# Four places in a queue: when a gated-DeltaNet layer's values, gate row, keys' turns and a late rsqrt are issued

## The chip, the cores and the metric

The kernel runs on one core of one Trainium2 chip. The metric is the device time of one execution in microseconds (us). The engines go by the profile's names: PE is TensorE (PEld its weight loads), DVE VectorE, ACT ScalarE, POOL GpSimd, SP the engine whose queue issues most DMAs. Each engine works through its own queue in order, so an instruction that waits holds up all that stands behind it on that engine.

## What is computed

One layer of a diffusion backbone over 1024 latent tokens and 256 context tokens of width 1024. After a modulated norm, one input projection feeds eight heads of neighbourhood attention and four heads of a gated DeltaNet. A branch's output is multiplied by a gate, and both go through one output projection. What the change touches is the DeltaNet's front, cut here to its core:

```python
def gdn_qkv(qkv, conv_w):                 # qkv: columns of the input projection
    qkv = short_conv(qkv, conv_w)         # 5 taps per channel, then silu
    q, k, v = jnp.split(qkv, ...)         # 4 heads of 128 each
    return l2norm(q), l2norm(k), v        # then axial rope on latent q and k

# gated_delta_chunked, per head and chunk of 64 tokens
a = jnp.where(lower, (k * beta) @ k.T * decay, 0.0)
t_inv = solve_triangular(eye + a, eye)    # unit lower triangle
u, w = t_inv @ (v * beta), t_inv @ (k * beta * exp(gc))
qk = (q @ k.T) * decay                    # then a scan over the chunks
```

## The kernel before

The kernel has stages one behind the other. Up to some 115 us it builds the modulated norm `hh`/`hl` (the input split in two parts, so that a product is three matmuls: high by high, low by high, high by low) and begins the projections. From there to some 435 us runs `phase2`, in which the DeltaNet's heads 0 to 3 are prepared. From 435 to 552 us, which is called the merges' stage below, the small inverses are put together (`tz`, `tu`, `tm`) between the last projections (`na_proj` of pairs 2 and 3). Attention and scan follow up to some 780 us and the output product up to the end.

In `phase2` each head h takes the steps of a string. Q and K (`conv`): 48 matmuls each of 512 columns of the projection (`gpl`), and for keys the context's (`gpc`); then five taps on ACT and DVE (`acc`, line 887), a tanh on ACT (line 888) and the multiply that ends the silu on DVE (line 889). F (`delta_front`) is the decay matrix of the head before: `em` from a DMA through ACT, `pk` on PE, `pm` and `qe` on DVE. Then `"RVppTppUB"`: R is the residual gate's row (`res_gate`: `parg` on PE, a copy `growg` on ACT, the product `pg` on PE, line 427), V the values' conv, p one piece of other projections as filler, T (`qk_tok`) the turning of queries and keys into token rows (`tp` on PE, line 909), with a copy and squares on ACT (line 915), one rsqrt on POOL (`rq_y_g`, lines 169 and 170: an add and a power) and the rotation on POOL and DVE (lines 921 to 933; `tok`). U turns the values (`vtp`, line 826), B (`qk_back`) turns the rotated keys and queries back (`tb`, line 944). From head 2 on a generator of triangular inversions is woven in: `tb`/`vb` on DVE (lines 1078 and 1081), 31 steps of two instructions each, over group 0 (head 0 and half of head 1) in head 2 and over group 1 in head 3. Group 2 follows in the merges' stage (`ab_vv`). The name `tb` thus stands for a DVE scratch at line 1078 and a PSUM tile at line 944.

The program's text is not the order of the queues. A scheduler with a simulated timeline places the instructions of each engine by priority and by what its model says of readiness; `self.order(r, before)` adds an edge without a semaphore, so that r comes behind another instruction of the same queue. Tiles come from pools with a count of buffers: two for `xp`, three for `acc`, three for the PSUM tiles `tp`, `pg` and `pk` together, two for `pm` and for `qe`.

The only place in which the kernel before uses such an edge on PE in the projections is in the stage ahead of `phase2`: `self.after` holds one matmul of a projection behind the last of the products that pick rows for the norm (`pa`, line 310).

## Time and profile before

| | |
|---|---|
| median of 3 runs | 872.3 us (871.33 to 875.08) |
| profiled execution | 871.71 us, of which the trace's span is 869.9 us |
| mean granted PE clock | 0.972 |
| PE busy | 824.9 us (95%) |
| PE's weight loads | 696.4 us (80%) |
| DVE busy | 502.7 us (58%) |
| ACT busy | 417.3 us (48%) |
| POOL busy | 357.3 us (41%) |
| chain that ended last | PE 59%, DVE 16%, DMA 15%, issue 4% |

A row of a timeline reads: start, duration, engine, line, operation, output and inputs, how many instructions are drawn together, and in brackets the idle time of the engine just before it with what ended it. The granted clock (PEclk) is the share of full speed that TensorE got in a stretch: 1.00 is 2.4 GHz and 0.50 is 1.2 GHz. The 1.8 us between span and execution lie around the traced work and belong to no stage.

### The profile page before, as it was taken

What the parts mean: (1) busy time and instruction counts of PE and PEld (TensorE: products, weight loads), DVE (VectorE), ACT (ScalarE), POOL (GpSimd) and SP (SyncE); (2) the same over time, 40 slices, a digit from 0 to 9 for tenths busy, and PEclk for the clock granted to TensorE, in tenths of its full rate; (3) what the DMA queues carried; (4) which work ended last, traced back from release to release, by engine and by line L of the source; (5) the groups of instructions that cost most, each with busy time, mean ns of one, the idle gap of its engine ahead of it and who ended that gap; (6) DMA issues with size and microseconds to landing.
All of it is one profiled execution on the core that took longest, in us unless ns stands there. A gap on an engine that the chain in (4) does not pass through costs nothing.

```text
span 869.9 us, 16461 instructions
## 1 busy us (share of the span) xinstructions
PE 824.9 (95%) x6082; PEld 696.4 (80%) x6082; DVE 502.7 (58%) x1051; ACT 417.3 (48%) x1087; POOL 357.3 (41%) x430
## 2 busy tenths in 40 slices
PE   6999999999999989989898999899999999999996
PEld 3678887888788867769786788788898988878885
DVE  3444455536743699859935964456666655653342
ACT  5244334753664643355314334366666667734210
POOL 2224141453462553328262100655757559624110
PEclk9999999999999999989998999699999999999999
DMA  8778352255444825562597569995967925134251
GB/s 340 265 259 295 97 170 88 73 170 168 142 157 154 221 85 170 176 171 81 176 283 226 160 187 290 419 258 149 313 179 262 259 78 191 49 110 133 87 184 69
DMA packets 86054, 159.65 MB, mean 184 GB/s; under 512 B 18373, under 2 KB 45334, under 8 KB 83798
## 3 DMA queue, kind: packets, MB, share of 16 engines
q1 hardware_dynamic: 78486, 144.94, 53.0%
q10 hardware_dynamic: 7488, 13.67, 5.1%
q8 instruction: 48, 0.79, 0.4%
q14 instruction: 32, 0.26, 0.1%
HBM read 109.51 MB, written 52.42 MB: 186 GB/s over the span
## 4 chain that ended last, share of the span: by engine, by line
PE 59%; DVE 16%; DMA 15%; issue 4%; ACT 2%; POOL 2%; SPq 1%; DVEq 0%; POOLq 0%; ACTq 0%
PE py L1369 3%; PE py L1370 3%; PE py L1371 3%; DVE tb L1078 3%; DVE vb L1081 3%; PE pa L1260 2%; PE pz L463 2%; PE pz L468 2%; PE pz L467 2%; PE po L789 2%; DMA wada<-in_w_ada 2%; PE pa L1271 2%; PE po L784 2%; DMA pm_dram<-pm 2%; PE tr L772 2%
## 5 line engine op out<-in xcount | busy, mean ns | idle before, releaser
L759 ACT ACTIVATE pt<-pt,nm 128x544 f32<-128x544 f32 (+1 forms) x64 | 50.5, 790 | 37.5 <-DVE nm L758 37.0
L758 DVE CUSTOM_DVE_ANT_0 pt<-sc,gm 128x544 f32<-128x544 f32 (+1 forms) x64 | 49.4, 771 | 32.2 <-PE sc L754 25.8
L742 POOL TENSOR_TENSOR gm<-gt,mk 128x288 f32<-128x288 f32 (+1 forms) x48 | 46.5, 971 | 29.1 <-DVE nm L758 28.8
L1232 POOL TENSOR_SCALAR kd<-kt,kd 128x128 f32<-128x128 f32 x72 | 42.7, 605 | 20.5 <-PE pa L1271 19.9
L1020 ACT ACTIVATE em<-em,gc 128x128 f32<-128x128 f32 x80 | 25.5, 391 | 34.9 <-DMA em<-gc_dram 29.7
L467 PE MATMUL pz<-hl,wh_gz 128*128 128x512 f32 x96 | 38.6, 402 | 0.0
L463 PE MATMUL pz<-hh,wh_gz 128*128 128x512 f32 x96 | 38.3, 399 | 0.0
L468 PE MATMUL pz<-hh,wl_gz 128*128 128x512 f32 x96 | 38.2, 398 | 0.0
L476 PE MATMUL pv<-wh_nv,hh 128*128 128x264 f32 x128 | 35.5, 296 | 2.0 <-ACT hh L265 1.7
L477 PE MATMUL pv<-wh_nv,hl 128*128 128x264 f32 x128 | 36.8, 292 | 0.0
L1431 DVE TENSOR_TENSOR finv<-py,ggb 128x512 f32<-128x512 f32 x16 | 10.9, 689 | 43.2 <-ACT finv L1430 43.1
L478 PE MATMUL pv<-wl_nv,hh 128*128 128x264 f32 x128 | 35.6, 287 | 0.0
L1274 DVE SCALAR_TENSOR_TENSOR s<-s,egl,pa 128x128 f32<-128x128 f32 x64 | 19.6, 344 | 27.2 <-PE pa L1271 27.2
L1039 POOL TENSOR_SCALAR_AFFINE_SELECT qe<-qe 128x256 f32<-128x256 f32 x32 | 25.5, 800 | 24.1 <-DVE qe L1038 24.1
L887 DVE SCALAR_TENSOR_TENSOR acc_v<-xp_v,cols,acc_v 128x1282 f32<-128x1282 f32 x16 | 29.1, 1817 | 10.9 <-ACT acc_v L885 10.6
L1078 DVE TENSOR_TENSOR tb<-ab,vb 120x31 f32<-120x31 f32 (+15 forms) x62 | 30.2, 487 | 8.7 <-DMA ab<-ab_dram 7.1
L1137 POOL COPY tm<-ld 32x320 f32<-32x320 f32 x16 | 7.4, 464 | 65.0 <-DMA tm_dram<-tm 27.1
L1430 ACT ACTIVATE finv<-py 128x512 f32<-128x512 f32 x16 | 9.5, 597 | 48.6 <-PE py L1371 30.5
L1238 POOL TENSOR_SCALAR vb<-v,beta 128x128 f32<-128x128 f32 x40 | 24.2, 604 | 20.4 <-DVE y L1244 17.2
L772 PE MATMUL tr<-c,pt 128*96 128x128 f32 (+1 forms) x192 | 31.8, 275 | 0.0
L1035 DVE SCALAR_TENSOR_TENSOR pm<-pk,beta,em 128x128 f32<-128x128 f32 x80 | 23.5, 342 | 14.0 <-PE pk L1028 10.9
L770 ACT COPY tcx<-tc 128x256 f32<-128x256 f32 x64 | 23.4, 366 | 16.2 <-PE tc L768 15.8
(432 smaller groups left out, 2852.7 us busy)
## 6 DMA issues: line engine op xcount, KB each, us to landing
wada<-in_w_ada SPq DMA_DIRECT2D x16, 512.0 KB
em<-gc_dram SPq DMA_DIRECT2D x20, 256.0 KB
pm_dram<-pm SPq DMA_DIRECT2D x20, 256.0 KB
tm_dram<-tm SPq DMA_DIRECT2D x8, 640.0 KB
kk<-qk_dram SPq DMA_DIRECT2D x16, 320.0 KB
tm<-tm_dram SPq DMA_DIRECT2D x4, 1280.0 KB
kq_dram<-kq SPq DMA_DIRECT2D x4, 1152.0 KB
kq<-kq_dram SPq DMA_DIRECT2D x4, 1152.0 KB
```

What stands on the lines that cost most here:

```text
L463: r = nc.tensor.matmul(ps, wh, xh, start=(k == 0), stop=False)
L467: nc.tensor.matmul(ps, wh, xl, start=False, stop=False)
L468: nc.tensor.matmul(ps, wl, xh, start=False, stop=(k == KC - 1))
L476: nc.tensor.matmul(ps, xh, wh, start=(k == 0), stop=False)
L477: nc.tensor.matmul(ps, xl, wh, start=False, stop=False)
L478: nc.tensor.matmul(ps, xh, wl, start=False, stop=(k == KC - 1))
L742: r = nc.gpsimd.tensor_tensor(self.gm[hh][:, 384 - n:384].rearrange("p (n c r) -> p n c r", c=nco, r=4), gv, self.mk[:, mo:mo + n].rearran ...
L758: nc.vector.tensor_tensor_reduce(pt[:, 384 - n:], sc[:, 512 - n:768], gm[:, 384 - n:], -1.0, 3.0e38, ALU.add, ALU.min, nm)
L759: self.last_exp = nc.scalar.activation(pt[:, 384 - n:], pt[:, 384 - n:], AF.Exp, bias=nm, scale=-1.0, accum_out=sums[:, ct, hh:hh + 1]).in ...
L772: self.pe(nc.tensor.transpose(pl[:m, rc * P:(rc + 1) * P], pt[:, 384 + (rc - 3) * m:384 + (rc - 2) * m], self.ident))
L1078: nc.vector.tensor_tensor(t3, bc(ab[:, 0:m, m:m + 1], [r, m, n]), bc(vb[:, m:m + 1, m:], [r, m, n]), ALU.mult)
L1232: r = nc.gpsimd.tensor_scalar(kd[d], kt_[:, t, :], self.kd[:, h, d, t:t + 1], None, ALU.mult)
```

## The change

Five things are edited, four of them by an edge in a queue.

1. The values' silu is split off `conv` (`late=True` gives back a function) and issued in a step of its own, "v", behind T. Its tanh is put behind the last of the head's squares on ACT (`last_sq`). The multiply that ends it is now line 910.
2. `res_gate` becomes a generator. Its product `pg` is issued in a step "r" behind V, with an edge behind the last matmul of the projections issued by then (`last_mm`).
3. The turns back (`tb`, now line 969) get an edge behind the `last_mm` of that moment.
4. The rsqrt over all heads' queries (`rho`), which only the scan uses, gets an edge behind the fourth head's `rq_y_g3` on POOL.
5. A wrapper `mm` issues the projections' matmuls and keeps the name of the last one; with it the use of `self.after` is gone, so that the edge in the stage ahead of `phase2` is gone as well.

No operation is added or removed on any engine. The scheduler sets all queues anew, so more rows move than those named.

```diff
+    def mm(self, *a, **k):
+        r = self.nc.tensor.matmul(*a, **k)
+        self.last_mm = r.ins.name
+        if self.seq:
+            self.pe(r)
...
-    def rsqrt(self, pool, x, n, tag, eps):
+    def rsqrt(self, pool, x, n, tag, eps, behind=None):
         y = pool.tile([P, n], F32, name=f"rq_y_{tag}", tag=f"rq_y{n}")
-        self.nc.gpsimd.tensor_scalar(y, x, eps, None, ALU.add)
-        self.nc.gpsimd.tensor_tensor(y, y, bc(self.mhalf, [P, n]), ALU.pow)
+        r = self.nc.gpsimd.tensor_scalar(y, x, eps, None, ALU.add)
+        if behind:
+            self.order(r, behind)
+        self.last_rsqrt = self.nc.gpsimd.tensor_tensor(y, y, bc(self.mhalf, [P, n]), ALU.pow).ins.name
...
         nc.scalar.copy(rows, par)
+        yield
...
-        nc.tensor.matmul(pg[:1, :256], self.sel[:, 0:1], rows, start=True, stop=True)
+        self.order(nc.tensor.matmul(pg[:1, :256], self.sel[:, 0:1], rows, start=True, stop=True), self.last_mm)
...
-            r = nc.tensor.matmul(ps, wh, xh, start=(k == 0), stop=False)
-            if self.after:
-                self.order(r, self.after)
-                self.after = None
+            self.mm(ps, wh, xh, start=(k == 0), stop=False)
...
-                for c in "RVppTppUB":
+                for c in "RVrppTvppUB":
...
-        nc.scalar.activation(xp[:, s0:1282], av, AF.Tanh, scale=0.5)
-        nc.vector.scalar_tensor_tensor(av, xp[:, s0:1282], 1.0, av, ALU.add, ALU.mult)
+        def silu():
+            r = nc.scalar.activation(xp[:, s0:1282], av, AF.Tanh, scale=0.5)
+            if late:
+                self.order(r, self.last_sq)
+            nc.vector.scalar_tensor_tensor(av, xp[:, s0:1282], 1.0, av, ALU.add, ALU.mult)
...
+        behind = self.last_mm
...
-                nc.tensor.transpose(pb[:, t, :], tok[:, t, :], self.ident)
+                self.order(nc.tensor.transpose(pb[:, t, :], tok[:, t, :], self.ident), behind)
...
-            self.rho = self.rsqrt(self.cp, self.ssq.rearrange("p h t -> p (h t)"), 32, "rho", 4 * EPS)
+            self.rho = self.rsqrt(self.cp, self.ssq.rearrange("p h t -> p (h t)"), 32, "rho", 4 * EPS,
+                                  self.last_rsqrt)
```

DVE in head 2, before: the multiply that ends the values' silu (`acc_v2`, line 889) stands early among the inversion steps of group 0 (`tb0`, `vb0`).

```order
L1078 TENSOR_TENSOR tb0_2755<-ab0_2752,vb0_2754 120x156
L1081 TENSOR_TENSOR vb0_2754<-vb0_2754,tb0_2755 120x26x6
L889 SCALAR_TENSOR_TENSOR acc_v2_2769<-xp_v2_2768,acc_v2_2769 128x1282
L1078 TENSOR_TENSOR tb0_2755<-ab0_2752,vb0_2754 120x175
L1081 TENSOR_TENSOR vb0_2754<-vb0_2754,tb0_2755 120x25x7
```

DVE in head 2, after:

```order
L1106 TENSOR_TENSOR vb0_2746<-vb0_2746,tb0_2747 120x18x14
L1103 TENSOR_TENSOR tb0_2747<-ab0_2744,vb0_2746 120x255
L910 SCALAR_TENSOR_TENSOR acc_v2_2761<-xp_v2_2760,acc_v2_2761 128x1282
L1106 TENSOR_TENSOR vb0_2746<-vb0_2746,tb0_2747 120x17x15
L565 SCALAR_TENSOR_TENSOR st_z10_3131<-st_z10_3131,pz1_0_3106 128x512
L945 TENSOR_TENSOR tok2_0_0_2996<-tp2_0_0_2993,rq_y_g2_3029 128x256
```

The multiply has moved from behind the step of 156 elements to behind that of 255, past 17 instructions of the inversion, and stands now just ahead of the keys' `tok2`.

PE at the values' turns of head 2 (`vtp2_0`, `vtp2_2`), before: they stand right behind the last filler product `pz1_0`.

```order
L467 MATMUL pz1_0_3094<-hl_113,wh_gz1_4_3089 128x512
L468 MATMUL pz1_0_3094<-hh_112,wl_gz1_4_3090 128x512
L826 MATMUL vtp2_0_3129<-c128_60,acc_v2_2769 128x128 x2
L826 MATMUL vtp2_2_3135<-c128_60,acc_v2_2769 128x128 x4
L463 MATMUL gpl_q30_3212<-hh_112,wh_gq3_0_3197 128x512
```

PE at the same place, after:

```order
L157 MATMUL gpl_q30_3224<-hh_112,wh_gq3_4_3215 128x512
L157 MATMUL gpl_q30_3224<-hl_113,wh_gq3_4_3215 128x512
L843 MATMUL vtp2_0_3141<-c128_60,acc_v2_2761 128x128 x2
L843 MATMUL vtp2_2_3147<-c128_60,acc_v2_2761 128x128 x4
L157 MATMUL gpl_q30_3224<-hh_112,wl_gq3_4_3216 128x512
```

The turns have moved behind 23 of the 24 products `gpl_q30` of the next head's queries.

POOL in head 3, before: the power of `rho` stands ahead of both instructions of `rq_y_g3`, which the keys' `tok3` needs.

```order
L169 TENSOR_SCALAR rq_y_rho_5749<-ssq_1091 128x32
L933 TENSOR_TENSOR tok3_1_6_3781<-tok3_1_6_3781,rot3_16_3795 128x512
L170 TENSOR_TENSOR rq_y_rho_5749<-rq_y_rho_5749,mhalf_67 128x32
L169 TENSOR_SCALAR rq_y_g3_3836<-ss3_3799 128x10
L1192 TENSOR_TENSOR rho2_5752<-rq_y_rho_5749 128x32
L170 TENSOR_TENSOR rq_y_g3_3836<-rq_y_g3_3836,mhalf_67 128x10
```

POOL in head 3, after:

```order
L957 TENSOR_TENSOR tok3_1_6_3785<-tok3_1_6_3785,rot3_16_3799 128x512
L177 TENSOR_SCALAR rq_y_g3_3840<-ss3_3803 128x10
L180 TENSOR_TENSOR rq_y_g3_3840<-rq_y_g3_3840,mhalf_67 128x10
L177 TENSOR_SCALAR rq_y_rho_5749<-ssq_1091 128x32
L180 TENSOR_TENSOR rq_y_rho_5749<-rq_y_rho_5749,mhalf_67 128x32
L1218 TENSOR_TENSOR rho2_5752<-rq_y_rho_5749 128x32
```

The two instructions of `rq_y_g3` now come first. On DVE `acc_v3`'s multiply stands behind the step of 252 elements of group 1, where before it stood behind that of 156, and `tok3` follows one row later.

DVE at the start of the merges' stage, after: the transposes `vx`, `vd`, `ld` (32 by 32 blocks) of merges 0 and 1 stand ahead of the first step of group 2; before, they stand between its steps, from the fourth on.

```order
L538 TENSOR_TENSOR sl_k22_4461<-pk2_2_4435,sh_k22_4460 128x256
L1139 STREAM_TRANSPOSE vx0_4405<-vl0_4387 128x1024
L1140 STREAM_TRANSPOSE vd0_4403<-vx0_4405 128x640
L1141 STREAM_TRANSPOSE ld0_4404<-vd0_4403 128x640
L1139 STREAM_TRANSPOSE vx1_4607<-vl1_4388 128x1024
L1140 STREAM_TRANSPOSE vd1_4421<-vx1_4607 128x640
L538 TENSOR_TENSOR sl_k20_4641<-pk2_0_4615,sh_k20_4640 128x512
L1141 STREAM_TRANSPOSE ld1_4422<-vd1_4421 128x640
L1103 TENSOR_TENSOR tb2_qh0_4370<-ab_vv_4368 80x31
```

On PE the first merge's `tz0`, which reads `ld0`, has moved ahead by 33 products of the filler, and between the last merges stand 48 products of the filler where 21 stood.

## Rows read from the trace of the kernel before

**Rows 1.** The page's first part: busy us (share of the span) and instructions

```profile
PE 824.9 (95%) x6082; PEld 696.4 (80%) x6082; DVE 502.7 (58%) x1051; ACT 417.3 (48%) x1087; POOL 357.3 (41%) x430
```

**Rows 2.** Waits of PE, 300 to 440 us: us in total, times, longest

```profile
PE tb L944 <- DVE tok L921: 4.3, 2, 2.9
PE tp L909 <- ACT sq L915: 3.3, 1, 3.3
PE pg L427 <- ACT growg L421: 2.9, 1, 2.9
PE gpc_v L468 <- POOL wl_gv L449: 0.4, 1, 0.4
```

**Rows 3.** Stretches: length, busy us of PE, PEld, DVE, ACT, POOL, clock, DMA, GB/s

```profile
320.00:325.00 5.00, 5.00 (x20) 4.20 (x21) 4.93 (x4) 4.75 (x23) 4.54 (x7) 0.70 0.29 106
375.00:385.00 10.00, 10.00 (x31) 7.36 (x32) 4.19 (x5) 8.09 (x16) 2.84 (x2) 0.70 0.62 144
435.00:552.00 117.00, 108.57 (x1432) 90.51 (x1431) 66.98 (x146) 39.92 (x85) 30.80 (x45) 0.91 0.80 243
```

**Rows 4.** Timeline of ACT and PE around head 2's wait for the squares

```profile
317.94 1.27 ACT L888 ACTIVATE xp_v<-acc_v 128x1282 f32<-128x1282 f32 x1 [7.44 <-DVE acc_v L887]
...
319.93 1.12 PE L909 MATMUL tp<-c,acc_k 128*128 128x128 f32 x4 [3.26 <-ACT sq L915]
...
326.21 0.82 PE L826 MATMUL vtp<-c,acc_v 128*128 128x128 f32 x6
...
327.33 0.39 PE L468 MATMUL gpl_q<-hh,wl_gq 128*128 128x512 f32 x1
327.56 0.39 PE L463 MATMUL gpl_q<-hh,wh_gq 128*128 128x512 f32 x1
...
334.03 0.41 PE L944 MATMUL tb<-c,tok 128*128 128x128 f32 x2 [1.44 <-DVE tok L921]
```

**Rows 5.** Timeline of DVE and POOL in head 2's inversion (group 0)

```profile
319.56 1.49 DVE L889 SCALAR_TENSOR_TENSOR acc_v<-xp_v,acc_v 128x1282 f32<-128x1282 f32 x1
320.96 1.42 DVE L1078 TENSOR_TENSOR tb<-ab,vb 120x175 f32<-120x175 f32 x1
...
326.50 0.38 DVE L1078 TENSOR_TENSOR tb<-ab,vb 120x207 f32<-120x207 f32 x1
...
332.19 0.42 DVE L1078 TENSOR_TENSOR tb<-ab,vb 120x255 f32<-120x255 f32 x1
...
322.22 1.30 POOL L933 TENSOR_TENSOR tok<-tok,rot 128x512 f32<-128x512 f32 x1
```

**Rows 6.** Timelines of DVE, PE and POOL in head 3

```profile
387.38 0.21 DVE L1078 TENSOR_TENSOR tb<-ab,vb 120x31 f32<-120x31 f32 x1 [3.74 <-DMA ab<-ab_dram]
...
401.02 2.58 DVE L889 SCALAR_TENSOR_TENSOR acc_v<-xp_v,acc_v 128x1282 f32<-128x1282 f32 x1
...
403.88 1.34 DVE L1078 TENSOR_TENSOR tb<-ab,vb 120x175 f32<-120x175 f32 x1
...
411.18 0.42 DVE L1081 TENSOR_TENSOR vb<-vb,tb 120x252 f32<-120x252 f32 x1
...
416.53 1.01 DVE L921 TENSOR_TENSOR tok<-tp,rq_y_g 128x256 f32<-128x256 f32 x2
...
407.75 0.82 PE L826 MATMUL vtp<-c,acc_v 128*128 128x128 f32 x6
...
404.98 5.55 POOL L170 TENSOR_TENSOR rq_y_rho<-rq_y_rho,mhalf 128x32 f32<-128x32 f32 x1
```

**Rows 7.** Timeline of PE ahead of `phase2`

```profile
53.55 0.75 PE L476 MATMUL pv<-wh_nv,hh 128*128 128x264 f32 x4 [0.94 <-ACT hh L265]
```

**Rows 8.** Timeline of DVE in the merges' stage

```profile
462.51 0.20 DVE L1078 TENSOR_TENSOR tb_qh<-ab_vv 80x31 f32<-80x31 f32 x1 [11.92 <-DMA ab_vv<-ab_dram]
...
465.40 1.25 DVE L1114 STREAM_TRANSPOSE vx<-vl 128x1024 f32<-128x1024 f32 x1 [1.07 <-DMA qk_dram<-sl_k]
...
467.32 1.26 DVE L1115 STREAM_TRANSPOSE vd<-vx 128x640 f32<-128x640 f32 x1
...
468.68 0.83 DVE L1116 STREAM_TRANSPOSE ld<-vd 128x640 f32<-128x640 f32 x1
...
510.51 0.19 DVE L1081 TENSOR_TENSOR ab_vv<-ab_vv,tb_qh 80x31 f32<-80x31 f32 x1
```

More of the change, by code (lines that the diff above doesn't have):

```diff
@@ L147, in __init__ @@
         self.gm = {}
-        self.gate = self.after = None
+        self.gate = self.last_pe = self.last_hh = None
+        self.seq = False
     def order(self, r, before):
@@ L431, in res_gate @@
         nc.sync.dma_start(self.gg_dram[:, n:n + 256], br[:, 0, :])
+        yield
     def load_w(self, pool, c0, n, tag, bufs=(3, 4, 4), halves=2, load=None, ks=None, dst=None):
@@ L462, in mm_chan @@
                 xh, xl = (v.rearrange("p (a t c) -> p t a c", a=8, t=4) for v in (xh, xl))
-            r = nc.tensor.matmul(ps, wh, xh, start=(k == 0), stop=False)
-            if self.after:
-                self.order(r, self.after)
-                self.after = None
-            nc.tensor.matmul(ps, wh, xl, start=False, stop=False)
-            nc.tensor.matmul(ps, wl, xh, start=False, stop=(k == KC - 1))
+            self.mm(ps, wh, xh, start=(k == 0), stop=False)
+            self.mm(ps, wh, xl, start=False, stop=False)
+            self.mm(ps, wl, xh, start=False, stop=(k == KC - 1))
     def mm_tok(self, ps, w, c0, n, xsel, ks=range(KC)):
@@ L475, in mm_tok @@
             xh, xl = xsel(k)
-            nc.tensor.matmul(ps, xh, wh, start=(k == 0), stop=False)
-            nc.tensor.matmul(ps, xl, wh, start=False, stop=False)
-            nc.tensor.matmul(ps, xh, wl, start=False, stop=(k == KC - 1))
+            self.mm(ps, xh, wh, start=(k == 0), stop=False)
+            self.mm(ps, xl, wh, start=False, stop=False)
+            self.mm(ps, xh, wl, start=False, stop=(k == KC - 1))
     def nat_tok(self, t):
@@ L802, in phase2 @@
             self.fill, self.ready = self.projections(cv), []
-            kq, conv, toks = {}, {}, {}
+            kq, conv, toks, gate_row = {}, {}, {}, None
             def step(h, c):
+                nonlocal gate_row
                 if c in "QKV":
                     i = "QKV".index(c)
-                    conv[c] = self.conv(cv, ps, 4 * i + h, f"{'qkv'[i]}{h}", i > 0)
+                    conv[c] = self.conv(cv, ps, 4 * i + h, f"{'qkv'[i]}{h}", i > 0, c == "V")
+                    if c == "V":
+                        conv[c], conv["v"] = conv[c]
+                elif c == "v":
+                    conv.pop("v")()
+                elif c == "r":
+                    next(gate_row)
                 elif c == "p":
@@ L815, in step @@
                 elif c == "R":
-                    self.res_gate(cv, ps, h)
+                    gate_row = self.res_gate(cv, ps, h)
+                    next(gate_row)
                 elif c == "T":
@@ L862, in projections, with conv @@
         yield from self.na_proj(pool, self.ps, [2, 3])
-    def conv(self, cv, ps, chunk, tag, has_ctx):
+    def conv(self, cv, ps, chunk, tag, has_ctx, late=False):
         nc = self.nc
@@ L887, in conv @@
             nc.vector.scalar_tensor_tensor(av, xp[:, s0 + tap:s0 + tap + 1282 - s0], wc(tap), av, ALU.mult, ALU.add)
-        nc.scalar.activation(xp[:, s0:1282], av, AF.Tanh, scale=0.5)
-        nc.vector.scalar_tensor_tensor(av, xp[:, s0:1282], 1.0, av, ALU.add, ALU.mult)
+        def silu():
[3 more added lines that the diff above has]
+            nc.vector.scalar_tensor_tensor(av, xp[:, s0:1282], 1.0, av, ALU.add, ALU.mult)
+        if late:
+            return acc, silu
+        silu()
         return acc
@@ L914, in qk_tok @@
                     sq = cv.tile([P, P], F32, name=f"sq{h}_{which}{t0 + t}", tag="sq", bufs=1)
-                    nc.scalar.activation(sq, pt[:, t, :], AF.Square,
-                                         accum_out=ss[:, t0 + t - first:t0 + t - first + 1])
+                    self.last_sq = nc.scalar.activation(sq, pt[:, t, :], AF.Square,
+                                                        accum_out=ss[:, t0 + t - first:t0 + t - first + 1]).ins.name
                 pts.append((t0, n, pt, tok))
```

## Prediction

> **What bounds the kernel now.** The page's busy times come first: TensorE works 95% of the span and no other engine over 58% [rows 1], so time is won only where TensorE stands still or runs at half its clock. The list of its waits says where that is in the stage that the change edits: four waits of 3.3, 2.9, 1.4 and 2.9 us and one of 0.4, together 10.9 us [rows 2]. Behind two of them it also loses clock: 320 to 325 us was granted 0.70, so 1.5 us are lost, and 375 to 385 us 0.70, so 3.0 [rows 3]. The merges' stage has more to give: in 117 us TensorE is busy for 108.6, so it stands for 8.4, and at a mean clock of 0.91 it loses another 10.5 [rows 3]. Then each wait is followed to the engine that ends it. The 3.26 us at 319.93 wait for squares on ACT, and ACT had stood for 7.44 us at the values' tanh, which waited for DVE [rows 4]. The 2.86 us at 417 wait for `tok3` at 416.53, and the rsqrt that it needs stood on POOL behind a power of 5.55 us for `rho`, which only the scan uses [rows 2, 6]. So all four orders aim at real waits. What the reader should look at next is DVE: in head 2 it has no gap from 319.56 to past 332, in head 3 none from 387.38 to 418 [rows 5, 6].
>
> **The change part by part.** I sum against the profiled execution of 871.7 us, which lies 0.6 under the median.
>
> *Ahead of `phase2`.* With the edge of `self.after` gone, six products of 0.23 us [rows 4] come before the row-picking matmuls, so these and the `hh` that follows from them on ACT are 1.4 us later. TensorE already waits 0.94 us for an `hh` there [rows 7]. Nothing new covers it: +1.2 us, from 0 (the six products fill a hole) to 2.5 (a second wait, for the context's norm, whose transposes also move ahead).
>
> *Head 2.* The squares no longer stand behind the tanh: the 3.26 us and the 1.5 of clock go. The 1.44 us at the turns back go too, since `tok2` is ready at about the old time and TensorE reaches its turns later in its queue. But the tanh takes the multiply of `acc_v2` along, and the order puts that behind 17 more instructions of the inversion, with `vtp2` waiting for it. Before, DVE worked without a gap through the multiply and the step of 255, which began at 332.19; the same work in another order ends where it ended, so `acc_v2` is ready near 332.5 in place of 321 [rows 5]. TensorE reached the values' turns at 326.21 [rows 4]; less 3.26 and 1.5 that is 321.5, plus 23 products of 0.23 us it is 326.8. A new wait of up to 332.5 − 326.8 = 5.7 us. Its lower bound comes from four steps from 320.96 to 326.50 that took 1.4 us each where the next took 0.38: POOL's 1.3 us additions ran beside them [rows 5]. If those fell elsewhere, 4.1 us would go and 1.6 be left. I take 5.0, near the upper end, as POOL has the same work in the same stretch, and 1.5 of clock behind it, as behind the 3.26. Head 2: −3.26 − 1.5 − 1.44 + 5.0 + 1.5 = **+0.3** (−4.6 to +1.0).
>
> For those slow steps the Trainium skill has a rule: in "SBUF — State Buffer", section "Who interferes with whom", a DVE instruction with two SBUF inputs contends with a GpSimd instruction that reads SBUF, and one of them blocks for the other's whole instruction. The trace agrees (1.42 us beside 0.38) [rows 5]. The rule speaks against this change: an order that puts one more instruction which PE needs behind a row of such steps puts it behind POOL's work as well. By it the wait is 5.7 us, and without it 1.6.
>
> *Head 3.* `pg` stands later by some six us of products, and `growg` should be there: −2.95 and its 3.0 of clock, and the 0.44 of `gpc_v`, whose cast on ACT no longer stands behind `em`. `rq_y_g3` is freed of the 5.55 us power, so the 2.86 go. What is late next is again the values' multiply. DVE's work from 387.38 ended with the step of 252 at 411.6; in place of 2.5 us beside POOL the multiply costs 1.4, one tap of 1.5 now fills the gap before 387.38, and the last `vb` of 0.4 comes behind it: ready at 411.6 − 1.1 − 1.5 − 0.4 = 408.6 [rows 6]. TensorE reached `vtp3` at 407.75; less 2.95, 3.0 and 0.44, plus 0.5 for four filler products ahead of it and 0.3 from head 2, that is 402.1. A wait of up to 6.5 us; were the five slow steps there fast (1.34 against some 0.35), 1.6. I take 5.5 with 1.5 of clock. Head 3: −2.95 − 3.0 − 0.44 − 2.86 + 5.5 + 1.5 = **−2.2** (−7.6 to +0.4).
>
> So up to 430 us the TensorE gains 2.2 − 0.3 − 1.2 = 0.7 us: the waits change their names more than their sum.
>
> *The merges' stage.* Here DVE and the DMAs lead, and they gain. `tok3` follows the multiply at 409 and not 416.5, and the way from it (turns back, `pk`, `pm`, two stores in flight) brings the load of `ab_vv` some 5 us forward, as the round trips of `pm` take back a third. DVE waited 11.92 us for that load; the six transposes of merges 0 and 1 (2 × (1.25 + 1.26 + 0.83) = 6.7 us) stood behind it, between the steps, and now stand in front of it [rows 8]. Group 2, ended at 510.7, would end near 510.7 − 5 − 6.7 = 499. The last merge followed it by 41 us, so that chain would end at 540 and not 552; TensorE with 8.4 + 10.5 us of idle and lost clock in this stage [rows 3] can follow, and with 48 filler products among the last merges in place of 21 it has 27 × 0.23 = 6 us of work to put into their waits. Against it: merges 1 to 3 wait for each other's `tm` stores, which no order shortens. Of the 11.7 us I take 60%: **−7** (0 to −12).
>
> Sum: 1.2 + 0.3 − 2.2 − 7 = −7.7, so 864.0 in the profiled execution and **864.5** by the median.
>
> **The rivals.** *The waits go and no others come.* POOL's work falls beside other DVE instructions and the values are ready almost in time: 1.2 − 4.6 − 7.6 − 7 = −18, **854**. For it: the scheduler put the turns there by a timeline in which they fit. Against it: the slow steps in both heads [rows 5, 6].
>
> *The merges give nothing.* The chain of `tm` stores and the load of `ab_vv`, which collides with the loads of `vl` and `pmf`, set the end as before, or the gain is waited out in front of attention: −0.7, **872**. For it: the DMAs are at 0.80 in that stage [rows 3].
>
> *Slower: the first merge is too early.* `tz0` stands 33 products, 7.6 us, further forward on TensorE. It needs `ld0`, which came at 469.5 [rows 8] from loads that the same queue issues behind the inversion of group 1. If these come no earlier, TensorE waits up to 7.6 us longer there, at the end of a stretch in which it also paid the upper ends: 1.0 + 0.4 + 2.5, less what the last merges give back. It decides from some 4 us of new wait at `tz0` on: +6, **878**.
>
> **How the numbers follow.** My forecast has 0.47 (its own range 860 to 869), waits gone 0.17, merges give nothing 0.23, too early 0.13. A measurement here tells some 0.5%, or 4.4 us, from no change, so faster means under 868. Faster: 0.43 of the forecast's 0.47 and 0.17, so 0.60; slower over 876.7: most of 0.13 and a little of the third, 0.14; the rest, 0.26, the same. The range of 853 to 876 leaves out half of the second case's lower side and most of the last case's upper one, about 0.17.
>
> **What would show it.** Right: no wait of TensorE for `sq`, `growg` or `tok`; in their place one of 3 to 6 us for `acc_v` (line 910) at each of `vtp2` and `vtp3`, with the clock down behind them; the first step of group 2 some 5 us earlier and its last some 11; attention beginning near 544. Wrong: no wait at `vtp` (then the first rival), inversion steps on DVE of 0.4 us throughout, or a first `sc` of attention still at 552. The forecast fails most easily at the 60%: it rests on stores that the order does not show.

## The result, and the profile after

The kernel after takes **875.65 us** (median of 20 runs, 871.93 to 878.54), the kernel before on the same chip 872.31 (20 runs, 868.12 to 875.15). The ratio is 1.0035 with an interval of [1.0022, 1.0048]: 3.3 us slower, where 864.5 was forecast. The time lies inside the forecast's range, at its upper end, and on the other side of no change.

The profiled execution of after was the lowest of its 20, 871.93 us with a span of 869.8, level with before's 869.9. So its trace tells where time moved, and not the whole of the 3.3 us.

In the heads the waits are the ones that the prediction named. The list of TensorE's waits from 300 to 440 us (us in total, times, longest), which answers to [rows 2], has no `sq`, `growg` or `tok` any more:

```profile
PE vtp L843 <- DVE acc_v L910: 8.9, 2, 5.9
PE pv L157 <- POOL wl_nv L461: 1.4, 1, 1.4
```

The timelines of ACT, DVE and PE in heads 2 and 3 of after, which answer to [rows 4 to 6]:

```profile
321.52 1.31 DVE L1103 TENSOR_TENSOR tb<-ab,vb 120x156 f32<-120x156 f32 x1
321.80 1.27 ACT L907 ACTIVATE xp_v<-acc_v 128x1282 f32<-128x1282 f32 x1
322.86 0.32 DVE L1106 TENSOR_TENSOR vb<-vb,tb 120x156 f32<-120x156 f32 x1
...
330.78 1.49 DVE L910 SCALAR_TENSOR_TENSOR acc_v<-xp_v,acc_v 128x1282 f32<-128x1282 f32 x1
...
332.32 1.54 PE L843 MATMUL vtp<-c,acc_v 128*128 128x128 f32 x6 [5.86 <-DVE acc_v L910]
...
408.38 1.49 DVE L910 SCALAR_TENSOR_TENSOR acc_v<-xp_v,acc_v 128x1282 f32<-128x1282 f32 x1
...
409.92 0.88 PE L843 MATMUL vtp<-c,acc_v 128*128 128x128 f32 x6 [3.02 <-DVE acc_v L910]
```

The tanh is done at 323.1, but the multiply starts 7.7 us later, because DVE first works through the inversion steps that the order put ahead of it. These steps are short, 0.32 to 0.42 us each from 322.86 on. The long steps of [rows 5] came beside POOL's work again, but earlier in the inversion: four instructions between 317.48 and 322.83 took 1.37, 0.80, 1.28 and 1.31 us.

Now the stretches (length, busy us of PE, PEld, DVE, ACT, POOL, clock, DMA share, GB/s). First two of the kernel before, which [rows 3] does not have:

```profile
50.00:60.00 10.00, 9.06 (x57) 7.79 (x56) 4.28 (x11) 6.78 (x14) 1.28 (x2) 1.00 0.88 294
300.00:435.00 135.00, 123.90 (x726) 106.81 (x725) 116.50 (x213) 62.28 (x171) 58.84 (x52) 0.96 0.48 144
```

and the same of after, with the stage of the merges and the stretch behind `vtp2`:

```profile
50.00:60.00 10.00, 8.00 (x42) 7.22 (x42) 3.94 (x9) 4.25 (x9) 1.29 (x2) 0.83 0.83 280
300.00:435.00 135.00, 124.03 (x722) 107.93 (x721) 119.52 (x220) 62.10 (x170) 61.90 (x57) 0.95 0.49 148
332.00:342.00 10.00, 9.68 (x43) 8.19 (x44) 9.89 (x19) 3.46 (x7) 2.68 (x4) 0.81 0.48 148
435.00:552.00 117.00, 109.85 (x1439) 90.82 (x1437) 67.97 (x139) 40.42 (x86) 28.95 (x41) 0.92 0.77 230
```

Read PE's busy time against the length: from 300 to 435 us TensorE stood for 135 − 123.90 = 11.1 us before and for 11.0 after. The four kinds of wait in [rows 2] became the two listed above and 0.5 us of small ones, and the sum stayed. From 50 to 60 us it stands 1.1 us longer and has a clock of 0.83 in place of 1.00. In the merges' stage it stands for 7.2 us in place of 8.4, at 0.92 in place of 0.91; 7 us of gain were forecast there, and in this trace the attention behind it begins 1.3 us earlier (below).

The timeline ahead of `phase2`, which answers to [rows 7]: the eight `pa` now have nothing between them and the products that need the `hh` they lead to.

```profile
49.13 0.40 PE L157 MATMUL pk<-hh,wqk_l 128*128 128x512 f32 x1
49.36 0.95 PE L320 MATMUL pa<-c,rows 128*128 128x2 f32 x8
52.31 1.16 PE L157 MATMUL pv<-wh_nv,hh 128*128 128x264 f32 x4 [2.00 <-ACT hh L275]
```

And the merges' stage. SP's queue, one wait of that queue (us in total, times, longest), and DVE's timeline, which answers to [rows 8]:

```profile
442.52 1.24 SPq L1071 DMA_DIRECT2D ab_dram<-pm_dram  x2
443.86 1.98 SPq L1120 DMA_DIRECT2D pmf<-pm_dram  x4
445.94 9.58 SPq L1131 DMA_DIRECT2D vl<-yd  x8
455.56 1.31 SPq L1071 DMA_DIRECT2D ab_dram<-pm_dram  x2
...
460.19 0.41 SPq L1080 DMA_DIRECT2D ab_vv<-ab_dram  x1
```

```profile
SPq L1131 <- DMA pmf<-pm_dram: 6.7, 4, 1.9
```

```profile
458.88 1.25 DVE L1139 STREAM_TRANSPOSE vx<-vl 128x1024 f32<-128x1024 f32 x1 [13.35 <-DMA vl<-yd]
...
466.26 0.17 DVE L1103 TENSOR_TENSOR tb_qh<-ab_vv 80x31 f32<-80x31 f32 x1
...
508.92 0.19 DVE L1106 TENSOR_TENSOR ab_vv<-ab_vv,tb_qh 80x31 f32<-80x31 f32 x1
```

The load of `ab_vv` and the first `sc` of the attention in the kernel before:

```profile
451.28 0.30 SPq L1055 DMA_DIRECT2D ab_vv<-ab_dram  x1
...
552.38 0.58 PE L751 MATMUL sc<-kk,qh 128*128 128x256 f32 x1
```

and that `sc` in after:

```profile
551.09 0.58 PE L760 MATMUL sc<-kk,qh 128*128 128x256 f32 x1
```

The load of `ab_vv` was to come 5 us earlier. It was issued at 460.19, against 451.28 before. Half of the stores into `ab_dram` stand on SP behind eight loads of `vl`, and these wait 6.7 us for the loads of `pmf`. So the merges 0 and 1 start earlier (`vx` at 458.88 for 465.40), group 2 later (466.26 for 462.51), and its end is earlier by 1.6 us (508.92 for 510.51), where 11.7 had been worked out. The 11.7 had two parts. The transposes that no longer stand between the steps gave 5.3 of the 6.7 counted for them: from first step to end the group took 42.9 us in place of 48.2. The other part, a first step 5 us earlier, turned into one 3.75 later. The late load does not explain that alone: DVE came out of the transposes only at 466.3, and these had waited 13.35 us for `vl`. The first `sc` of the attention stands at 551.09 and was at 552.38; it was to stand near 544.

### The profile page after: what moved, and what is told of

It is laid out like the page before. It is cut to its first block, busy times and chain, and to the rows that moved or that the text cites. A ratio compares the mean times of both kernels' runs of the same rounds, so it can differ in the third digit from the quotient of the medians.

```text
span 869.8 us, 16465 instructions
## 1 busy us (share of the span) xinstructions
PE 824.4 (95%) x6082; PEld 699.2 (80%) x6082; DVE 505.9 (58%) x1051; ACT 419.1 (48%) x1087; POOL 358.4 (41%) x430
## 4 chain that ended last, share of the span: by engine, by line
PE 75%; DVE 12%; DMA 8%; issue 2%; ACT 2%; SPq 1%; POOL 0%; DVEq 0%; POOLq 0%; ACTq 0%
PE pz L157 8%; PE pv L157 5%; PE gpl_k L157 5%; PE pq L157 5%; PE gpl_q L157 5%; PE gpl_v L157 4%; PE py L1395 3%; PE py L1396 3%; PE py L1397 3%; PE pa L1286 3%; PE po L798 2%; PE pa L1297 2%; PE po L793 2%; PE sc L763 2%; PE tr L781 2%
## 5 line engine op out<-in xcount | busy, mean ns | idle before, releaser
L157 PE MATMUL pz<-hh,wh_gz 128*128 128x512 f32 x96 | 40.1, 418 | 0.0
L157 PE MATMUL pv<-wh_nv,hh 128*128 128x264 f32 x128 | 37.4, 312 | 2.8 <-ACT hh L275 2.2
L157 PE MATMUL pv<-wl_nv,hh 128*128 128x264 f32 x128 | 37.8, 303 | 1.7 <-POOL wl_nv L461 1.4
L157 PEld LDWEIGHTS pv<-wh_nv,hh 128*128 128x128 f32 x128 | 25.8, 210 | 7.3 <-ACT hh L275 5.1
```

Source lines behind the costliest of these rows:

```text
L157: r = self.nc.tensor.matmul(*a, **k)
```

## The experiments

Every kernel was timed beside the kernel before. "Clock" is the mean granted clock over all timed runs of the kernel.

| kernel | median us | before beside it | ratio | clock |
|---|---|---|---|---|
| after | 875.65 | 872.31 | 1.0035 [1.0022, 1.0048] | 0.970 |
| e1: after without order 1 | 872.25 | 871.91 | 1.0009 [0.9985, 1.0034] | 0.978 |
| e2: before with order 1 alone | 870.82 | 871.91 | 0.9982 [0.9961, 1.0003] | 0.973 |
| e3: before with order 4 alone | 874.24 | 871.91 | 1.0014 [0.9998, 1.0031] | 0.973 |
| e4: after with the order ahead of `phase2` put back | 872.22 | 871.91 | 1.0001 [0.9980, 1.0022] | 0.972 |
| e5: before without that order | 878.53 | 871.89 | 1.0073 [1.0044, 1.0101] | 0.968 |
| e6: e4, `ab_vv` loaded first | 875.32 | 871.89 | 1.0027 [1.0004, 1.0050] | 0.968 |
| e7: e4, values' multiply earlier on DVE | 874.49 | 871.89 | 1.0020 [0.9997, 1.0044] | 0.968 |
| e8: e6 and e7 together | 873.56 | 871.89 | 1.0015 [0.9990, 1.0040] | 0.969 |
| e9: e8, stores of `tm` before the scan's loads | **867.11** | 873.12 | **0.9935** [0.9912, 0.9957] | 0.972 |
| e10: e1 with the order ahead of `phase2` put back | 871.04 | 873.12 | 0.9980 [0.9959, 1.0002] | 0.978 |
| e11: after once more | 874.56 | 873.12 | 1.0019 [1.0000, 1.0039] | 0.971 |

### Taking the change apart: e1 to e4

e1 leaves the values' silu where it was:

```diff
-                    conv[c] = self.conv(cv, ps, 4 * i + h, f"{'qkv'[i]}{h}", i > 0, c == "V")
-                    if c == "V":
-                        conv[c], conv["v"] = conv[c]
+                    conv[c] = self.conv(cv, ps, 4 * i + h, f"{'qkv'[i]}{h}", i > 0)
...
-                for c in "RVrppTvppUB":
+                for c in "RVrppTppUB":
```

> The changed kernel with its first edit taken back: the values' tanh and its multiply are issued in V again, without the edge behind the squares; gate row, turns back, late rsqrt and the lost edge ahead of phase2 stay. Theory A (the new waits of PE for acc_v at the values' turns, 5.9 and 3.0 us in the trace after, with the half clock behind them, cost what the other edits save): both vtp waits are gone, the 3.3 us wait for the squares of head 2 is back with about 1.5 us of clock, the 2.9 us waits for growg and tok stay away; the time is about 5 us under the changed kernel and 1 to 3 us under the kernel before, 869 to 871 us. Theory B (the end is set by the merges' stage, where the load of ab_vv was issued 9 us later than before behind the loads of vl; waits in the heads are absorbed there): since the load stands in the same place here, the time stays within 1.5 us of the changed kernel's 875.7.

e2 makes that edit alone in the kernel before (the string becomes `"RVppTvppUB"`), cut here to the silu:

```diff
-        nc.scalar.activation(xp[:, s0:1282], av, AF.Tanh, scale=0.5)
-        nc.vector.scalar_tensor_tensor(av, xp[:, s0:1282], 1.0, av, ALU.add, ALU.mult)
+        def silu():
+            r = nc.scalar.activation(xp[:, s0:1282], av, AF.Tanh, scale=0.5)
+            if late:
+                self.order(r, self.last_sq)
+            nc.vector.scalar_tensor_tensor(av, xp[:, s0:1282], 1.0, av, ALU.add, ALU.mult)
```

> The kernel before with the first edit alone (values' tanh behind the squares, multiply with it). The order of the merges' stage stays as before on PE, DVE and SP. Theory A: the waits of 3.3 and 1.4 us in head 2 go, waits for acc_v of about 5.5 us at vtp2 and 1 to 3 us at vtp3 come, with half clock behind them; the waits for growg (2.9) and tok (2.9) in head 3 stay: 1 to 4 us over the kernel before, 873 to 876 us. Theory B: the ab_vv load stands in front of the vl loads as before, so the time is within 1 us of the kernel before, 872.3.

e3 is the kernel before with `rho` behind the fourth head's rsqrt, and nothing else:

```diff
-            self.rho = self.rsqrt(self.cp, self.ssq.rearrange("p h t -> p (h t)"), 32, "rho", 4 * EPS)
+            self.rho = self.rsqrt(self.cp, self.ssq.rearrange("p h t -> p (h t)"), 32, "rho", 4 * EPS,
+                                  self.last_rsqrt)
```

> The kernel before with the fourth edit alone (rho's rsqrt behind the fourth head's). PE's wait for tok at 417 us (2.9) goes, and head 3's turns back, pk and pm stand 20 to 30 products earlier. The scheduler also moves four vl loads ahead of the ab_vv load and the first merge 17 products ahead on PE. Theory A: 2.9 us and 1 to 3 us of the merges' stage are won: 866 to 869.5 us. Theory B: the loads ahead of ab_vv cost what is won: 871 to 873 us.

e4 is the kernel after with the one edge back that the wrapper had dropped (`last_r` is the matmul that `mm` issued last):

```diff
-        self.gate = self.last_pe = self.last_hh = None
+        self.gate = self.last_pe = self.last_hh = self.after = None
...
+            if self.after:
+                self.order(self.last_r, self.after)
+                self.after = None
```

> The changed kernel with the edge that was lost ahead of phase2 put back (the first matmul of a projection behind the row-picking products); all four other edits stay, and from phase2 on all orders are those of the changed kernel. The trace after shows a wait of PE for hh of 2.0 us where before had 0.9, and a clock of 0.74 and 0.92 in the ten us from 50 to 60, where before had 1.00. If that is a steady cost: 2 to 3.5 us under the changed kernel, 872 to 873.5 us, level with the kernel before. If it is the chance of one execution: within 1 us of the changed kernel's 875.7.

e1, e2 and e3 lie within 0.2% of the kernel before, and each interval holds 1. So neither order 1 nor order 4 by itself is worth a time that these runs can tell; orders 2 and 3 were never run alone. The expectations were missed on both sides: e2 came out under both of its theories (870.8), e3 over both (874.2, where 866 to 869.5 was the hope), and e1 between its two; e4 alone came as expected. The waits tell what order 1 does. In e1 the old wait is there, in e2 the new one stands in its place (the lists of PE's waits, e1 and then e2):

```profile
PE tp L931 <- ACT sq L937: 3.7, 2, 3.2
```

```profile
PE vtp L830 <- DVE acc_v L896: 9.6, 2, 5.9
```

e4 has all four orders and takes the time of the kernel before (1.0001). Its stretches ahead of `phase2` and in the heads:

```profile
50.00:60.00 10.00, 9.54 (x56) 8.06 (x56) 4.95 (x12) 6.31 (x13) 1.28 (x2) 1.00 0.89 310
300.00:435.00 135.00, 123.79 (x714) 107.37 (x713) 120.03 (x225) 61.88 (x168) 61.90 (x57) 0.95 0.48 150
```

In the heads it stands as long as after does (11.2 us), so it is not there that it is faster. From 50 to 60 us it is busy for 1.5 us more than after and has the full clock, and its wait for `hh` is the shorter one:

```profile
52.24 0.76 PE L157 MATMUL pv<-wh_nv,hh 128*128 128x264 f32 x4 [0.46 <-ACT hh L275]
```

By the ratios after is 0.34% over e4, some 3 us, which is all that the change costs: the four announced orders come to nothing together that these runs can tell, and the fifth edit is the loss.

All thirteen traces say the same of the stage ahead of `phase2`. TensorE's order is the same in all of them up to the first products `pv` with `hh` and a little beyond. From there to the first `gpl_q` of `phase2`, in e4 and then in after:

```profile
42.53 0.77 PE L157 MATMUL pv<-wh_nv,hh 128*128 128x264 f32 x4
...
112.34 0.40 PE L157 MATMUL gpl_q<-hh,wh_gq 128*128 128x512 f32 x1
```

```profile
41.15 0.77 PE L157 MATMUL pv<-wh_nv,hh 128*128 128x264 f32 x4
...
113.89 0.40 PE L157 MATMUL gpl_q<-hh,wh_gq 128*128 128x512 f32 x1
```

That is 69.8 us with the edge and 72.7 without it. The nine traces with the edge (before, e2, e3, e4, e6 to e10) take 69.8 to 70.8 us, the four without it (after, e1, e5, e11) 72.0 to 72.9. So the lost edge costs 1.2 to 3.1 us there, 2.4 by the means. Some of it comes behind the wait: the scheduler also moved some forty products between 65 and 100 us.

### The lost edge alone: e5, e10, e11

e5 takes only that edge out of the kernel before, e10 puts it back into e1, with the lines shown for e4, and e11 is after again.

```diff
-            if self.after:
-                self.order(r, self.after)
-                self.after = None
```

> The kernel before with one line fewer: the order that puts the six first products of the projections behind the row-picking matmuls ahead of phase2 is left out, none of the four announced orders is made. Theory A (the lost order is the whole steady cost of the change: 875.65 after, 872.2 with the order put back): about 875, ratio 1.003 to 1.005; in the stretch 50 to 60 us TensorE waits some 2 us for hh in place of 0.94 and is granted less than full speed behind it, while the heads' waits (tb 4.3, tp 3.3, pg 2.9) stay as in the kernel before. Rival B (the order costs nothing by itself, it only does together with the moved work): 872, ratio within 1.000 +- 0.0015. Rival C (my forecast's price for it, 1.2 us): 873.

> The kernel after without the first order (the values' tanh stands where it stood before) and with the order ahead of phase2 put back; so the gate row's product, the turns back and rho alone. Theory A (the lost order ahead of phase2 costs 3 to 6 us in whatever kernel it is lost): e1, which lacked it, took 872.25, so this takes 866 to 869 and is faster than the kernel before. Rival B (what the lost order costs hangs on the rest, and e1 had none of it to give back): 871 to 873.

> The kernel after once more, for its time beside the others of this call and for a second trace, since the first trace was taken of its fastest run. 875 to 876, ratio 1.003 to 1.005, and a span of 872 to 875 in the trace. Where its trace is longer than the first one's 869.8 us, theory A has the difference in lost clock and in the wait for hh between 50 and 100 us; the rival has it in the stretch in front of attention, 500 to 560 us, where stores and loads collide.

e5 is slower than the kernel before by 6.6 us, an interval that excludes 3.3 (0.44% to 1.01%, 3.8 to 8.8 us). Its wait ahead of `phase2` is the one foretold:

```profile
53.57 0.75 PE L473 MATMUL pv<-wh_nv,hh 128*128 128x264 f32 x4 [2.00 <-ACT hh L265]
```

e10 against e1 gives the edge 1.0009 − 0.9980 = 0.29%, 2.5 us, with intervals that overlap. e10 was expected at 866 to 869 and came to 871. So the sign is the same in three pairs (6.6, 3.0, 2.5 us). That the edge costs something is shown by e5's time and by the traces ahead of `phase2`; that it costs all of the 3.3 us in after rests on e4, whose interval is 1.8 us to either side. e11 came to 1.0019, under the 1.003 to 1.005 that was expected, so the second measurement of the change is 1.7 us and not 3.3, and its interval only touches 1.

The same four kernels (after, e1, e4, e10) can be read the other way. Order 1 costs 0.26% from e1 to after and 0.21% from e10 to e4, nearly as much as the edge's 0.34 and 0.29, and taking it back also brings the time to the kernel before. But e2, which makes order 1 alone, is 0.18% under the kernel before. All these intervals overlap, so whether order 1 costs something beside the other edits is not shown.

e11's trace has the same stretch as the first trace of after: from 50 to 60 us 8.00 us busy at 0.83, and 10.1 us of waits at the two `vtp`; its attention begins at 553.2. It does not tell theory A from its rival by length, since its span of 870.6 us is again of a low run.

e5's own trace is of its lowest run as well (874.39 us) and shows a clock of 1.00 from 50 to 60 us. Over all its runs the mean clock was 0.968, against 0.9725 in the kernel before beside it: 0.5% of clock over a time of 872 us is some 4 us. Where in e5 that clock was lost no trace shows, and this part of the 6.6 us stays open. Nor is mean clock the same as time: e1 and e10 had 0.978 and were no 4 us faster than the kernel before. And e5 is not that edge alone in every queue: from 480 us on the scheduler has placed products among the merges in another order than in the kernel before, and its trace loses a further 1.3 us between 500 and 551. This rival for the part above 3.3 us was not tested.

### The merges' load first: e6

```diff
-        nc.sync.dma_start(ab[:n], self.ab_dram[120 * g:120 * g + n])
+        self.ab_load = nc.sync.dma_start(ab[:n], self.ab_dram[120 * g:120 * g + n]).ins.name
...
-            nc.sync.dma_start(pm[d][0:96], self.pm_dram[h][0:96, d])
+            self.order(nc.sync.dma_start(pm[d][0:96], self.pm_dram[h][0:96, d]), self.ab_load)
...
+            with tc.high_priority(offset=300):
+                next(gens[0])
```

(the loads of `vl` get the same edge, and the last lines have the load of `ab_vv` placed early)

> The kernel after with the order ahead of phase2 put back (as in e4, 872.2), and with the load of ab_vv issued on SP ahead of the loads of pmf and vl, where e4 has it behind them; the heads' stage is as in e4. Theory A (the merges' gain that I forecast failed because SP issued that load behind two other sets of loads): the load is issued some 8 us earlier, at 450 to 453 us, the first step of group 2 on DVE begins near 458 in place of 466, its last ends near 500, and the time falls by 3 to 7 us, to 865 to 869. Rival B (merges that come earlier only move filler products and TensorE has the same work left): the steps come earlier and the time stays at 871 to 873. Rival C (the transfers are what is short, so that pmf and vl come later by as much and merges 0 and 1 with them): tz0 comes 5 us or more later than at 462, a wait of TensorE for ld or vx grows by that, time 873 to 877.

SP, DVE and PE in e6's timeline:

```profile
447.51 0.32 SPq L1083 DMA_DIRECT2D ab_vv<-ab_dram  x1
...
453.95 0.20 DVE L1106 TENSOR_TENSOR tb_qh<-ab_vv 80x31 f32<-80x31 f32 x1 [8.94 <-DMA ab_vv<-ab_dram]
...
501.40 0.18 DVE L1109 TENSOR_TENSOR ab_vv<-ab_vv,tb_qh 80x31 f32<-80x31 f32 x1
...
471.18 2.34 PE L1157 MATMUL tz<-ld,pmf 32*32 32x32 f32 x80 [6.40 <-DVE ld L1145]
```

The load comes 12.7 us earlier and group 2 ends 7.5 us earlier, close to the 499 of the prediction. But merge 0 pays for it: its `tz` stands at 471.2 where it was at 462.4 in after, and the time is 875.3. The loads of `vl`, now behind that of `ab_vv`, are issued from 450.1 us on where it was 445.9, and the first `vx` stands 7.1 us later. That is rival C, with the mechanism of the transfers. An earlier group 2, bought in this way, is no gain; since merge 0 came later too, e6 does not tell what the earlier group 2 alone is worth.

### The values' multiply earlier on DVE: e7, and both: e8

e7 lets fewer inversion steps be issued ahead of "v" and puts the next step of the inversion behind the multiply:

```diff
-                for c in "RVrppTvppUB":
+                for i, c in enumerate("RVrppTvppUB"):
                     step(h, c)
-                    next(blocks, None)
+                    for _ in range((1, 1, 1, 1, 0, 0, 2, 2, 1, 1, 1)[i]):
+                        next(blocks, None)
...
+                if self.inv_behind and m > 1:
+                    self.order(t, self.inv_behind)
```

(`inv_behind` is the name of the values' multiply)

> The kernel after with the order ahead of phase2 put back (as in e4, 872.2), and with DVE's queue changed in heads 2 and 3: fewer inversion steps ahead of the multiply of acc_v, which goes ahead of 13 and 11 of them. The waits of TensorE for acc_v at vtp2 and vtp3 (5.9 and 3.0) then have nothing to wait for. Theory A (DVE's work bounds the heads' stage: whatever it does first, something that TensorE needs comes late): these two waits go, others of about the same sum come for the inversion's results or the turns (pm, em, ab), TensorE's idle time from 300 to 435 us stays at 11 to 12 us, time 871 to 874. Rival B (the place of the multiply in DVE's queue is the cause): idle time from 300 to 435 us falls by 5 to 8, time 864 to 868.

> The edits of e6 and e7 together, over the kernel after with the order ahead of phase2 put back. By theory A of e7 and rival B of e6 (waits and filler only change places): 871 to 874. If each gains by itself they should add up to 860 to 866. If only one gains, the time is that one's, within 2 us.

e7's multiply, `vtp2`, and two stretches:

```profile
326.31 1.48 DVE L914 SCALAR_TENSOR_TENSOR acc_v<-xp_v,acc_v 128x1282 f32<-128x1282 f32 x1
...
327.85 0.88 PE L846 MATMUL vtp<-c,acc_v 128*128 128x128 f32 x6 [0.57 <-DVE acc_v L914]
```

```profile
300.00:435.00 135.00, 130.34 (x772) 112.78 (x772) 121.88 (x222) 65.76 (x176) 70.47 (x61) 0.99 0.54 163
435.00:560.00 125.00, 102.04 (x1394) 84.97 (x1393) 65.12 (x139) 38.46 (x83) 28.85 (x42) 0.85 0.78 241
```

Here the theory falls that I had after e1 to e4, that DVE's work bounds the heads' stage and the waits only change their names. With the multiply in another place TensorE stands for 4.7 us from 300 to 435, not 11.2, at a clock of 0.99 and not 0.95: 6.5 us of standing and some 5 of clock gained in the heads. And the time is 874.5. In the next stage, counted to 560 us, it stands for 23.0 us, where e4 stood for 8.9. The gain is there and is given back, all of it and more, before the attention begins: that is at 557.5 us in this trace, which is of e7's longest run, and at 550.8 in e4's. Rival B had the mechanism and the wrong time, theory A nearly the time and the wrong mechanism.

e8 is the place to see where. Rows of its SP, DVE and PE waits, and of its chain of work that ended last (start, us, what):

```profile
529.42 0.58 SPq L164 DMA_DIRECT2D tm<-tm_dram  x1
530.09 0.38 SPq L1208 DMA_DIRECT2D tm_dram<-tm  x1
531.87 0.32 SPq L164 DMA_DIRECT2D v<-vt_dram  x1
...
532.77 0.38 SPq L1208 DMA_DIRECT2D tm_dram<-tm  x1
```

```profile
532.77 11.90 DMA tm_dram<-tm
```

```profile
544.76 0.48 DVE L1186 TENSOR_SCALAR tm<-tu 32x320 f32<-32x320 f32 x1 [5.40 <-DMA tm_dram<-tm]
```

```profile
PE tz L1195 <- DVE xo L1186: 7.0, 1, 7.0
```

All merges share a `tm` tile, so merge 3 may write it only when merge 2's store has landed. The store's second half took 11.9 us, with loads of the scan issued ahead of it and between the two halves; e9 below tests whether they are the reason. DVE, POOL and then TensorE stand for it, and no product is left to fill the time. e7's chain has the same store with 11.65 us. In after the same store came ahead of the loads and took 2.95 us (the chain of after):

```profile
542.46 2.95 DMA tm_dram<-tm
```

### The stores ahead of the loads: e9

```diff
+            r = nc.sync.dma_start(self.tm_dram[h][:, d], tm[d])
+            if h == 2:
+                self.tm2_store = r.ins.name
...
             self.load(dst, src)
+            self.order(self.last_r2, self.tm2_store)
```

(`load` keeps its DMA in `last_r2`; the load of `zg` gets the edge too)

> The kernel of e8 with one more order on SP: the loads of the scan (tm, v, kt, kq, qe, and zg) stand behind the two stores of tm of merge 2, where e8 issues some of them ahead of and between these stores; PE's, ACT's and POOL's orders are as in e8. In e8 the stores were issued at 530.1 and 532.8, merge 3 could write its tm and xo only at 544.8, and TensorE waited 7.0 + 2.9 us for that. Theory D (heads' and merges' gains are lost in front of attention because the stores that free tm queue with some 3 MB of scan loads): DVE writes tm of merge 3 some 5 to 8 us earlier, at 537 to 540, the wait for xo falls to 0 to 2 us, attention begins near 544 to 547 in place of 551, and the time falls by 4 to 7 us, to 866 to 869. Rival E (the scan's loads then come late and the attention and the scan wait for them instead): the wait for xo goes too, but waits for tm, kt or kq come behind 552 and the time stays at 872 to 874. Rival F (the transfers as a whole bound that stretch, whatever their order): tm is written no earlier than 543, time 872 to 875.

SP, the chain, DVE and the first `sc` of e9:

```profile
529.78 1.53 SPq L1208 DMA_DIRECT2D tm_dram<-tm  x2
```

```profile
530.99 7.09 DMA tm_dram<-tm
```

```profile
538.21 0.48 DVE L1186 TENSOR_SCALAR tm<-tu 32x320 f32<-32x320 f32 x1 [5.37 <-DMA tm_dram<-tm]
```

```profile
544.29 0.58 PE L763 MATMUL sc<-kk,qh 128*128 128x256 f32 x1
```

`tm` is written at 538.2 (544.8 in e8), the wait for `xo` is 0.9 us (7.0), the attention begins at 544.3 (550.9), and the time is 867.1: 0.65% under the kernel before, [0.43%, 0.88%]. That is theory D in place, size and time. The scan did not pay for its later loads: from 560 to 780 us TensorE stands for 7.7 us, and in e8 for 9.0. So rival E falls. e9 differs from e8 only in the order of a dozen DMAs in one queue, and it is the only kernel here whose interval lies clear of 1 on the faster side. The edge was not run on e4 by itself; there these loads stand behind both stores already (the stores are issued from 537.4 to 542.3 us, the loads from 543.1), so it would have nothing to move. So the gain over e4 would be that of e6 and e7, let through by the edge.

## Why the prediction was wrong, point by point

*What bounds the kernel.* Right about the waits that go and about the new ones. That TensorE's waits are the thing to win holds only where the stages behind can use the time: e7 won 6.5 us of them and no time. That a won wait can be spent was left to the rivals; the sum had one line for it ("merges give nothing", 872).

*Ahead of `phase2`, +1.2 (0 to 2.5).* The mechanism was right: the six products no longer lie behind `pa`, and the wait for `hh` is 2.00 us in place of 0.94. The term was mis-sized, for I counted lost clock behind the long waits of the heads and none behind this one. From 50 to 60 us busy time is 1.06 us less than before, and the clock of 0.83 in place of 1.00 costs 1.7 us of the ten: 2.8, and 3.2 against e4's trace. By the first `gpl_q` the traces without the edge are 2.4 us behind those with it on the mean, twice what I took and at the upper end of the range. That is most of the time that the change cost, as far as these runs can tell.

*Head 2, +0.3.* Right in the mechanism, a little small. The wait was 5.86 us (taken 5.0, at most 5.7), `acc_v2` ready at 332.3 (332.5), TensorE there at 326.5 (326.8), and the clock behind it 0.81 over ten us, 1.9 lost (1.5). With these the sum is −3.26 − 1.5 − 1.44 + 5.86 + 1.9 = +1.6, above the range. The lower bound of 1.6 us for the wait was read wrongly: it took the long steps (1.4 us) to matter only where the multiply jumps over them. In after these 17 instructions were short and the long ones stood ahead of them, and the multiply was as late, since DVE works through all of them without a gap.

*Head 3, −2.2.* Half right. (The upper end of its range, +0.4, does not follow from its terms: with the full 6.5 us of wait and 1.5 of clock they give −1.3.) `acc_v3` was ready at 409.9 (408.6) and all old waits were gone, but TensorE came to `vtp3` at 406.9 and not at 402.1: a wait of 1.4 us for a weight's low half on POOL (`wl_nv`) opened and the clock was lower than I had it (0.93 from 385 to 410 us, where before had 1.00). So the wait was 3.0 and not 5.5, and no time was won. Both heads together stand for as long as before, 11.0 us for 11.1. Why that sum is the same is not what I took from it: e7 shows that with DVE in another order TensorE stands for 6.5 us less.

*The merges, −7 (0 to −12).* **This step failed.** In place of some 7 us earlier the attention began 1.3 us earlier in the trace of after and 0.8 later in e11's. A first `sc` still near 552 is the sign of being wrong that the prediction named. It went wrong twice. First, I worked out when `ab_vv` could be loaded from the way of the data (`tok3`, `pm`, stores) and did not read SP's order between them: eight loads of `vl`, which wait for `pmf`, stood ahead of half the stores into `ab_dram`, so the load came 8.9 us later and not 5 earlier, and the transposes that went ahead of the first step waited for `vl` themselves. Second, the assumption behind it was false that an earlier group 2 pays by itself: e6 moved its end by 7.5 us and got nothing, though it also made merge 0 late; e7 and e8 brought the last merge's `vx` from 519.5 to 511.7 and 506.0 and got nothing, until e9 freed `tm`. In the chain of after group 2 and the load of `vl` lead only up to 526 us; from there to the attention it runs over TensorE's remaining products and the store of `tm`, and in e8 that store took back most of what the first part had won.

*The rivals.* "The waits go and no others come" fell with the two waits for `acc_v`. "Merges give nothing" came nearest, at 872 with 0.23; with the lost edge at 2.4 and not 1.2 it gives 873. "Too early" did not happen as told: `tz0` stood 7 us earlier and waited 3.8 us for `ld` in place of 1.6. But its kind of mechanism, a stage that starts earlier and meets the transfers, is what e6 to e8 show.

*What the trace hides.* Its 869.8 us are level with before's 869.9, though 2.8 us are lost from 50 to 60. About 1 us is made good in the merges' stage, and some two more at the start: from 20 to 30 us the clock was 0.91 in the trace of after and 0.70 in that of before. TensorE's order there is the same in all the kernels, and e4, e10 and e11 had 0.83, 0.71 and 0.83, so this is a difference of runs and not of kernels. e11's trace, 0.7 us longer than before's, begins the attention 0.8 us later than before, at 553.2.

## What to carry to other kernels

A won wait is worth something only if the next shared thing is free earlier too: before counting a gain, follow each step that comes earlier into the queue of its DMAs, and ask which store or load now stands in front of it. When several edits move time without winning any, look where the last of them is given back (here one store behind a set of prefetches), and put the store that frees a tile ahead of loads that nobody waits for yet. And look at what an edit drops: the one order that went with the rewriting cost more than the four new ones together brought.

## What the runs showed of the hardware that was not expected

- The last store of merge 2's `tm` (640 KB) took 2.95 us to land in after, 6.80 in before and 7.09 in e9, where the scan's loads were issued within a microsecond behind it, and 11.90 in e8, with loads ahead of it as well. Standing ahead of the loads won 4.8 us from e8 to e9. The rest of the difference from after is not only the loads behind it: in before and e9 the store's two halves were issued within 1.6 us, in after 4.8 us apart.
- The clock behind an equal wait was not equal. After the wait of 2.0 us for `hh` the traces of after and e11 had 0.83 from 50 to 60 us, those of e1 and e5 1.00.
- Over the runs of one kernel the time often went with the mean granted clock: correlations of −0.6 over the 20 runs of after and −0.8 to −0.9 in e1, e4, e5 and e8, though only −0.2 to −0.4 in e3, e7 and e11. The 20 runs of after lie 6.6 us apart, twice the 3.3 us in question, so at this size the trace of one run says little about a median.
